# Bias tables, weights and one DMA queue: three edits to a three-layer hybrid network on one core

## The chip, the cores and the metric

The kernel runs on one NeuronCore of a Trainium2 chip. The metric is the device time of one execution in microseconds (us). TensorE (PE) multiplies matrices into eight PSUM banks of 128 partitions by 512 f32 words. VectorE (DVE) and ScalarE (ACT) do the elementwise work, GpSimd (POOL) a little of it, and SyncE (SP) only starts transfers. Transfers run on the core's 16 DMA engines; SP's transfers form one queue (q1 in the profile), POOL's another (q0).

## The reference

Two blocks in a row, on 512 tokens of width 1024 (528 in the first block, which puts 16 meta tokens ahead):

```
layer 0: h += 0.5*swiglu(norm(h)); h += diff_attention(norm(h)) @ w_out; h += 0.5*swiglu(norm(h))
layer 1: the same with dsa_attention: index scores -> top_k keys -> attention on those keys
second block: x += 0.5*swiglu(norm(x))
              x += (ssm branch + dilated attention branch + memory cross attention branch) @ w_out
              x += 0.5*swiglu(norm(x)); out = norm(x)

def _swiglu(x, wi, wo):
    a, b = jnp.split(x @ wi, 2, axis=-1)          # 1024 -> 2 * 2816
    return (jax.nn.silu(a) * b) @ wo

act = relu(einsum("bqhd,bsd->bqhs", qi, k_idx) * IDX_DIM ** -0.5)     # 8 heads of 64
score = einsum("bqh,bqhs->bqs", wi, act)
br_mem = memory_cross_attention(xq, rmsnorm(mem, mem_norm), xattn_w_kv) @ xattn_w_up
```

Both attentions of the first block add a bias that depends on the distance of key and query alone (a table of 16 heads); the dilated attention adds one of 12 heads. There are six swiglu layers in all; they hold most of the work.

## The kernel before

**Precision.** Every f32 operand is split into a high and a low part of type fp32r, and a product of two operands is three matmuls: high by high, low by high, high by low. The split of a weights tile is `loadw` (L82 to L92): SP loads 128x1024 words into `st` (tag "st", three buffers), ACT casts them into `wh` (L89), DVE subtracts to get `wl` (L91).

**A swiglu layer** (`sffn`, L315) has 22 chunks of 128 hidden columns, in four groups of 5, 5, 6 and 6. A chunk's first half needs two products of the input with a 1024x128 slice, one for `a` and one for `b`. Two chunks of the first group are computed plainly (`plain`); the other 20 (`quad`) cut the two products into a 2x2 scheme with seven products of half the depth, 12 matmuls each (L402), 84 in a quad. `a_parts` loads the slices `g` and `u`, `sums` builds the combined weights with DVE additions, and `step(i)` does product i and what follows it. Products 1 and 2 share a PSUM bank, 5 and 3, and 6 and 7; product 4 has its own. ACT copies products 1 and 5 to SBUF (L407, L409), and DVE adds copies and banks (L413, L415, L418, L422, L423), multiplies the two halves (L425), and splits the result into `gh` and `gl`. After the chunks of a group, `partial` (L242) multiplies them with eight tiles of `wo`, one for each 128 output columns (d = 0 to 7): 30 matmuls of 264 columns for a group of five at 528 tokens, 15 of 512 at 512 tokens. The result is added to h by DVE (L262). A `wo` tile of such a group is 128x640 words, 320 KB; a `wi` tile is 512 KB.

**Hooks.** After each of these eight steps a hook may run a piece of another computation, up to its next `yield`: the bias tables `bias_a` (in layer 0's first swiglu, here FFN0) and `bias_d` (in the second block's first, FFN4), and in FFN2 (layer 1's first) the memory norm `mem_norm` and then `ssm_in`. A bias function multiplies the small table with a one-hot matrix (L533, L556), DVE copies the product (L534, L557), POOL stores it to DRAM as `fA` or `fD`, and then POOL starts transfers DRAM to DRAM that write each head's row 128 times, two heads in one transfer: eight `kA<-fA` of 256 rows of 656 words (L538), six `kD<-fD` of 256 rows of 640 words (L562). The attentions later read skewed strips of `kA` and `kD`.

**Banks.** In a swiglu layer, all eight banks form one ring (`s.banks(m=...)`), for products and hooks alike.

**Index scores** (`mixer_b`, L991). Two heads of 64 stand in one tile of 128 partitions; each head's three matmuls contract 64 partitions, on the upper and the lower half of the array.

**Order.** The program is written in the order above; a scheduler with a timing model then orders each engine's instructions at build time, so that pieces of neighbouring chunks, steps and hooks mix. On the chip each engine and each queue keeps that order.

Of the kernel before, what the change touches and what calls it, by code (L numbers as in the profile page):

```python
# [34 lines left out]
class Kern:  # L35
# [278 lines left out]
    def sffn(s, T, x, fi, gnext, final=False, hooks={}, quarters=False, w0=None):  # L314
# [7 lines left out]
        s.banks(m=list(range(8)))  # L322
        with ExitStack() as es:
# [30 lines left out]
            def quad(f):  # L354
# [29 lines left out]
                done = set()  # L384
# [6 lines left out]
                def step(i):  # L391
                    b = bank[i]
                    first = i not in (2, 3, 7)
                    if b not in st:
                        st[b] = s.bank()[:, :N]
                    B = st[b]
                    (wh, wl), o = W[i]
                    c = combo[i]
                    for k in range(4):
                        w = slice(o + k * 128, o + k * 128 + 128)  # L400
                        for z, (a, q) in enumerate(((wh, H), (wh, L), (wl, H))):
                            nc.tensor.matmul(B, a[:, w], q[c][:, k], start=first and k == 0 and z == 0,  # L402
                                             stop=k == 3 and z == 2, skip_group_check=not first)
                    cc = tile("cc", "cc", fp)
                    done.add(i)
                    if i == 1:
                        nc.scalar.copy(cc[:, :N], B)  # L407
                    elif i == 5:
                        nc.scalar.copy(cc[:, 264:264 + N], B)  # L409
                    elif i == 2:  # L410
                        nc.scalar.activation(tile("s", "sl")[:, :N], B, AF.Silu)
                    elif i == 6:
                        v.tensor_add(tile("s", "sl")[:, N:T], B, cc[:, :N])  # L413
                    elif i == 7:
                        v.tensor_add(tile("v", "sq")[:, N:T], B, cc[:, :N])  # L415
                    if i in (6, 3) and {6, 3} <= done:
                        q = st["s"][:, N:T]
                        v.tensor_add(q, st["z"], q)  # L418
                        nc.scalar.activation(q, q, AF.Silu)
                    if i in (7, 4) and {7, 4} <= done:  # L420
                        u = st["v"]
                        v.tensor_add(u[:, :N], st["w"], u[:, N:T])  # L422
                        v.tensor_add(u[:, N:T], u[:, N:T], cc[:, 264:264 + N])  # L423
                    if len(done) == 7:
                        v.tensor_mul(st["s"][:, :T], st["s"][:, :T], st["v"][:, :T])  # L425
                        gate(st["s"][:, :T])
                return a_parts, sums, step
            f0 = 0
            for grp, ng in enumerate((5, 5, 6, 6)):
# [5 lines left out]
                for j in range(2 if grp == 0 else 0, ng):  # L435
# [3 lines left out]
                    for i in (1, 2, 6, 4, 5, 7, 3) if f0 + j == 2 else (1, 6, 4, 5, 2, 7, 3):  # L439
                        step(i)  # L440
# [79 lines left out]
    def bias_a(s):  # L520
# [9 lines left out]
        for q in range(2):  # L530
            p = s.bank()
# [5 lines left out]
        for h in range(0, 16, 2):  # L537
            nc.gpsimd.dma_start(s.kA[h:h + 2], s.fA[h:h + 2].unsqueeze(1).to_broadcast((2, 128, 656)))  # L538

    def bias_d(s):  # L540
# [5 lines left out]
        oh, rt, f = a[:33, :640], a[:33, 640:652], b[:4, :640]  # L546
        nc.vector.memset(rt[32:33], NEG)
        nc.gpsimd.dma_start(rt[:32], s.I["rel_table"])
        for gr in range(3):
            nc.gpsimd.dma_start(oh, s.I["oh2"][:, gr])  # L550
            yield
            yield
            for q in range(2):
                p = s.bank()
                c = slice(q * 320, q * 320 + 320)
                nc.tensor.matmul(p[:4, :320], rt[:, gr * 4:gr * 4 + 4], oh[:, c], start=True, stop=True)  # L556
                nc.vector.tensor_copy(f[:, c], p[:4, :320])  # L557
            nc.gpsimd.dma_start(s.fD[gr * 4:gr * 4 + 4], f)
            yield
        yield  # L560
        for h in range(0, 12, 2):
            nc.gpsimd.dma_start(s.kD[h:h + 2], s.fD[h:h + 2].unsqueeze(1).to_broadcast((2, 128, 640)))  # L562
# [305 lines left out]
    def mixer_b(s, x, gnext, filler=None):  # L868
# [7 lines left out]
        with ExitStack() as es:  # L876
# [21 lines left out]
            with tc.tile_pool(name="bi", bufs=1) as bi:  # L898
                KH, KL = bi.tile([128, 528], F32R, name="kkh"), bi.tile([128, 528], F32R, name="kkl")
# [1086 lines left out]
```

## Time and profile before

| what | value |
|---|---|
| time of the runs, median of 3 | 3423.61 us (3417.93 to 3430.52) |
| time of the profiled execution | 3422.45 us |
| its span, first to last instruction | 3420.7 us |
| busy: PE, weight load, DVE, ACT, POOL | 97%, 90%, 76%, 48%, 8% |
| mean granted clock of TensorE | 0.984 |
| SP's queue, POOL's queue: share of the 16 DMA engines | 29.0%, 2.1% |

The span is what the profile can divide among engines; the 1.75 us between it and the profiled execution's time lie before and after the instructions. Busy shares are averages over stages that differ. A matmul's recorded duration overlaps that of its neighbours, so that the rate of matmuls says more than the busy share. A granted clock of 1.00 is 2.4 GHz, 0.50 is 1.2 GHz.

### The profile page before, as it was taken

What the parts mean: (1) busy time and instruction counts of PE and PEld (TensorE: products, weight loads), DVE (VectorE), ACT (ScalarE), POOL (GpSimd) and SP (SyncE); (2) the same over time, 40 slices, a digit from 0 to 9 for tenths busy, and PEclk for the clock granted to TensorE, in tenths of its full rate; (3) what the DMA queues carried; (4) which work ended last, traced back from release to release, by engine and by line L of the source; (5) the groups of instructions that cost most, each with busy time, mean ns of one, the idle gap of its engine ahead of it and who ended that gap; (6) DMA issues with size and microseconds to landing.
All of it is one profiled execution on the core that took longest, in us unless ns stands there. A gap on an engine that the chain in (4) does not pass through costs nothing. (4 is left out here: it accounts for less than half of the span.)

```text
span 3420.7 us, 60310 instructions
## 1 busy us (share of the span) xinstructions
PE 3304.6 (97%) x23692; PEld 3091.4 (90%) x23692; DVE 2614.7 (76%) x5463; ACT 1645.7 (48%) x3019; POOL 260.0 (8%) x443
## 2 busy tenths in 40 slices
PE   7999999999999999988999999999999899999998
PEld 7999899899999899977989999888998788898998
DVE  8777777799878797778868897787776555387776
ACT  5444577644445344455754444444455534344443
POOL 0100022100000000033310001000000000000000
PEclk9999999999999999999999999999999999999999
DMA  3532322223323433232212333243333243233332
GB/s 132 161 109 82 100 75 70 67 71 120 109 89 102 136 110 106 65 101 75 63 58 89 111 113 118 97 136 112 94 92 96 84 130 96 76 122 103 103 103 62
DMA packets 133646, 336.96 MB, mean 99 GB/s; under 512 B 27043, under 2 KB 39107, under 8 KB 133361
## 3 DMA queue, kind: packets, MB, share of 16 engines
q1 hardware_dynamic: 114336, 311.38, 29.0%
q0 software_dynamic: 19024, 21.72, 2.1%
q8 instruction: 186, 3.05, 0.4%
q14 instruction: 100, 0.81, 0.1%
HBM read 320.00 MB, written 24.35 MB: 101 GB/s over the span
## 5 line engine op out<-in xcount | busy, mean ns | idle before, releaser
L89 ACT CAST wh<-st 128x1024 fp32r<-128x1024 f32 (+5 forms) x385 | 318.9, 840 | 494.8 <-PE bank L111 281.4
L402 PE MATMUL bank<-xh,wh 128*128 128x264 f32 (+1 forms) x1920 | 545.1, 285 | 7.7 <-ACT wh L359 7.7
L402 PE MATMUL bank<-xh,wl 128*128 128x264 f32 (+1 forms) x1920 | 540.7, 284 | 6.8 <-DVE wl L360 6.8
L91 DVE TENSOR_TENSOR wl<-st,wh 128x1024 fp32r<-128x1024 f32 (+4 forms) x373 | 360.9, 974 | 148.0 <-ACT wh L89 146.8
L111 PE MATMUL bank<-gl,wh 128*128 128x264 f32 (+2 forms) x1674 | 456.6, 313 | 0.0
L113 PE MATMUL bank<-gh,wl 128*128 128x264 f32 (+2 forms) x1674 | 453.7, 313 | 0.0
L109 PE MATMUL bank<-gh,wh 128*128 128x264 f32 (+2 forms) x1674 | 453.2, 315 | 0.1
L111 PE MATMUL bank<-xl,wh 128*128 128x264 f32 (+3 forms) x1360 | 426.2, 318 | 4.4 <-DVE xl L182 3.1
L109 PE MATMUL bank<-xh,wh 128*128 128x264 f32 (+3 forms) x1360 | 416.2, 319 | 14.1 <-ACT xh L456 3.2
L113 PE MATMUL bank<-xh,wl 128*128 128x264 f32 (+3 forms) x1360 | 420.9, 315 | 0.0
L402 PE MATMUL bank<-xl,wh 128*128 128x264 f32 (+1 forms) x1440 | 408.2, 284 | 0.0
L402 PEld LDWEIGHTS bank<-xh,wh 128*128 128x128 f32 x1920 | 364.7, 190 | 11.5 <-ACT wh L359 10.3
L402 PEld LDWEIGHTS bank<-xh,wl 128*128 128x128 f32 x1920 | 362.8, 190 | 9.2 <-DVE wl L360 7.9
L402 PE MATMUL bank<-xq,wah 128*128 128x264 f32 (+1 forms) x1920 | 360.8, 284 | 0.3 <-ACT cc L407 0.3
L111 PEld LDWEIGHTS bank<-gl,wh 128*128 128x128 f32 x1674 | 289.1, 189 | 19.3 <-issue 0.5
L109 PEld LDWEIGHTS bank<-gh,wh 128*128 128x128 f32 x1674 | 287.1, 189 | 20.3 <-issue 1.6
L113 PEld LDWEIGHTS bank<-gh,wl 128*128 128x128 f32 x1674 | 287.1, 188 | 19.0 <-DVE wl L91 0.5
L402 PEld LDWEIGHTS bank<-xq,wah 128*128 128x128 f32 x1920 | 298.7, 189 | 1.8 <-ACT cc L407 0.5
L109 PEld LDWEIGHTS bank<-xh,wh 128*128 128x128 f32 (+1 forms) x1360 | 252.4, 190 | 36.2 <-DVE qs L457 4.0
L111 PEld LDWEIGHTS bank<-xl,wh 128*128 128x128 f32 (+1 forms) x1360 | 257.5, 190 | 21.7 <-DVE xl L182 3.8
L402 PEld LDWEIGHTS bank<-xl,wh 128*128 128x128 f32 x1440 | 273.2, 190 | 0.3
L113 PEld LDWEIGHTS bank<-xh,wl 128*128 128x128 f32 (+1 forms) x1360 | 257.0, 190 | 16.7 <-issue 1.4
(597 smaller groups left out, 7534.0 us busy)
## 6 DMA issues: line engine op xcount, KB each, us to landing
st<-in_wi SPq DMA_DIRECT2D x144, 512.0 KB, 4.2
fu<-in_wi SPq DMA_DIRECT2D x120, 512.0 KB, 3.8
st<-in_wo SPq DMA_DIRECT2D x96, 384.0 KB, 3.1
st<-in_wo SPq DMA_DIRECT2D x96, 320.0 KB, 3.0
st<-in_a_w_in SPq DMA_DIRECT2D x24, 512.0 KB, 3.7
st<-in_w_out SPq DMA_DIRECT2D x24, 512.0 KB, 3.7
st<-in_w_g SPq DMA_DIRECT2D x24, 512.0 KB, 3.6
strip<-kA SPq DMA_DIRECT2D x32, 264.0 KB, 2.8
```

Of the source, the lines that this page charges most:

```text
L89: nc.scalar.copy(wh[:rows, :n], st[:rows, :n])
L91: s.wl.tensor_tensor(wl[:rows, :n], st[:rows, :n], wh[:rows, :n].bitcast(F32), op=ALU.subtract)
L109: nc.tensor.matmul(p[:m], a, xh(k, t0, n), start=st, stop=False)
L111: nc.tensor.matmul(p[:m], a, xl(k, t0, n), start=False, stop=False)
L113: nc.tensor.matmul(p[:m], b, xh(k, t0, n), start=False, stop=en)
L402: nc.tensor.matmul(B, a[:, w], q[c][:, k], start=first and k == 0 and z == 0, stop=k == 3 and z == 2, skip_group_check=not first)
```

## The change

**Swiglu.** Products 6 and 7 now accumulate onto a bank ("y") that ACT has filled with a copy of product 1, and product 4 onto a bank ("w") that ACT has filled with a copy of the sum after product 7. In exchange for two more ACT copies, DVE does two additions and two half-width multiplications where it did five additions and one full-width multiplication. The order of products in a chunk becomes 1, 5, 6, 2, 7, 3, 4 (for chunk 2: 1, 2, 5, 6, 3, 7, 4). The ring has seven banks, and the eighth ("k") belongs to the hooks.

**Bias tables.** The `kA<-fA` and `kD<-fD` transfers, and the loads of `bias_d`'s inputs, are started by SP and not by POOL, so that they stand in the weights' queue; there is a `yield` after each pair of heads. **Memory norm.** `mem_norm` moves from FFN2 to FFN0, behind `bias_a`; its loads are SP's too. **Index scores.** The query tile of a head holds the high part in its own half and the low part in the other, so that two matmuls of 128 partitions do what three of 64 did; there are twice as many splits, of 64 partitions each.

```diff
-        s.banks(m=list(range(8)))
+        s.banks(m=list(range(7)), k=[7])
...
                 def step(i):
...
-                    first = i not in (2, 3, 7)
...
+                    B = room(bank[i])
...
+                            first = i in (1, 5) and k == 0 and z == 0
+                            nc.tensor.matmul(B, a[:, w], q[c][:, k], start=first, stop=k == 3 and z == 2,
+                                             skip_group_check=i not in (1, 5))
+                    cc, S, U = tile("cc", "cc", fp), tile("s", "sl"), tile("v", "sq")
                     if i == 1:
+                        nc.scalar.copy(room("y"), B)
+                    elif i == 5:
                         nc.scalar.copy(cc[:, :N], B)
-                    elif i == 5:
+                    elif i == 6:
                         nc.scalar.copy(cc[:, 264:264 + N], B)
                     elif i == 2:
-                        nc.scalar.activation(tile("s", "sl")[:, :N], B, AF.Silu)
-                    elif i == 6:
-                        v.tensor_add(tile("s", "sl")[:, N:T], B, cc[:, :N])
+                        nc.scalar.activation(S[:, :N], B, AF.Silu)
                     elif i == 7:
-                        v.tensor_add(tile("v", "sq")[:, N:T], B, cc[:, :N])
-                    if i in (6, 3) and {6, 3} <= done:
-                        q = st["s"][:, N:T]
-                        v.tensor_add(q, st["z"], q)
-                        nc.scalar.activation(q, q, AF.Silu)
-                    if i in (7, 4) and {7, 4} <= done:
-                        u = st["v"]
-                        v.tensor_add(u[:, :N], st["w"], u[:, N:T])
-                        v.tensor_add(u[:, N:T], u[:, N:T], cc[:, 264:264 + N])
-                    if len(done) == 7:
-                        v.tensor_mul(st["s"][:, :T], st["s"][:, :T], st["v"][:, :T])
-                        gate(st["s"][:, :T])
+                        nc.scalar.copy(room("w"), B)
+                        v.tensor_add(U[:, :N], B, cc[:, :N])
+                    elif i == 3:
+                        v.tensor_add(S[:, N:T], B, cc[:, 264:264 + N])
+                        nc.scalar.activation(S[:, N:T], S[:, N:T], AF.Silu)
+                    elif i == 4:
+                        v.tensor_mul(S[:, :N], B, S[:, :N])
+                        v.tensor_mul(S[:, N:T], S[:, N:T], U[:, :N])
+                        gate(S[:, :T])
...
-                    for i in (1, 2, 6, 4, 5, 7, 3) if f0 + j == 2 else (1, 6, 4, 5, 2, 7, 3):
+                    for i in (1, 2, 5, 6, 3, 7, 4) if f0 + j == 2 else (1, 5, 6, 2, 7, 3, 4):
...
         nc.gpsimd.dma_start(s.fA, f)
         yield
         for h in range(0, 16, 2):
-            nc.gpsimd.dma_start(s.kA[h:h + 2], s.fA[h:h + 2].unsqueeze(1).to_broadcast((2, 128, 656)))
+            nc.sync.dma_start(s.kA[h:h + 2], s.fA[h:h + 2].unsqueeze(1).to_broadcast((2, 128, 656)))
+            yield
...
-        for h in range(0, 12, 2):
-            nc.gpsimd.dma_start(s.kD[h:h + 2], s.fD[h:h + 2].unsqueeze(1).to_broadcast((2, 128, 640)))
+            nc.sync.dma_start(s.kD[h:h + 2], s.fD[h:h + 2].unsqueeze(1).to_broadcast((2, 128, 640)))
...
-                IH, IL = bi.tile([128, 4, 512], F32R, name="qih"), bi.tile([128, 4, 512], F32R, name="qil")
+                IQ = [bi.tile([128, 4, 512], F32R, name="qi%d" % a) for a in range(2)]
...
-                    s.split(IH[:, j], IL[:, j], ac[0][0])
+                    for b, (r, o) in enumerate(HALVES):
+                        s.split(IQ[b][r, j], IQ[b][o, j], ac[0][0][r])
...
-                            for z, (a, b) in enumerate(((IH, KH), (IH, KL), (IL, KH))):
-                                for q in range(2):
-                                    r = slice(q * 64, q * 64 + 64)
-                                    nc.tensor.matmul(ps[q][:, :w], a[r, j, i * 128:i * 128 + 128], b[r, k0:k0 + w],
-                                                     start=z == 0, stop=z == 2)
+                            for q in range(2):
+                                for z, b in enumerate((KH, KL[q])):
+                                    nc.tensor.matmul(ps[q][:, :w], IQ[q][:, j, i * 128:i * 128 + 128], b[:, k0:k0 + w],
+                                                     start=z == 0, stop=z == 1)
...
-            nc.gpsimd.dma_start(m, s.I["memT"][k:k + 2].rearrange("k p n -> p k n"))
+            nc.sync.dma_start(m, s.I["memT"][k:k + 2].rearrange("k p n -> p k n"))
...
-        x = s.sffn(528, x, 0, GI["ln_mix_0"], hooks=spread((0, 7, [s.bias_a()])), w0=w0)
+        x = s.sffn(528, x, 0, GI["ln_mix_0"], hooks=spread((0, 23, [s.bias_a(), s.mem_norm()])), w0=w0)
...
-        x = s.sffn(528, x, 2, GI["ln_mix_1"], hooks=spread((0, 23, [s.mem_norm(), s.ssm_in()])))
+        x = s.sffn(528, x, 2, GI["ln_mix_1"], hooks=spread((0, 23, [s.ssm_in()])))
```

The order of SP's transfers in FFN0, from the second `wo` tile of the first group on. Before, the group's `wo` tiles follow each other (the last six in one row), and the next group's `wi` tiles (`st` and `fu`) come after them:

```order
L367 DMA fu<-in_wi 128x1024
L86 DMA st<-in_wo 128x640
L367 DMA fu<-in_wi 128x1024
L86 DMA st<-in_wo 128x640 x6
L365 DMA st<-in_wi 128x1024 x3
```

Now, from the second `wo` tile on (L1410 loads the memory for `mem_norm`):

```order
L86 DMA st<-in_wo 128x640
L367 DMA fu<-in_wi 128x1024
L86 DMA st<-in_wo 128x640 x2
L536 DMA kA<-fA 256x1x656 x2
L86 DMA st<-in_wo 128x640
L536 DMA kA<-fA 256x1x656 x2
L86 DMA st<-in_wo 128x640
L536 DMA kA<-fA 256x1x656 x3
L86 DMA st<-in_wo 128x640
L536 DMA kA<-fA 256x1x656
L1410 DMA mm<-in_memT 128x2x256 x2
L86 DMA st<-in_wo 128x640
```

All eight tables stand between the `wo` tiles of the first group: two of them ahead of d = 4, four ahead of d = 5, seven ahead of d = 6, all eight ahead of d = 7 and of everything that the second group needs.

The same queue in FFN4, the second block's first swiglu layer, before, from the first `wo` tile:

```order
L86 DMA st<-in_wo 128x640
L367 DMA fu<-in_wi 128x1024
L86 DMA st<-in_wo 128x640
L367 DMA fu<-in_wi 128x1024
L86 DMA st<-in_wo 128x640 x6
```

And now (L563 loads a one-hot matrix):

```order
L86 DMA st<-in_wo 128x640
L367 DMA fu<-in_wi 128x1024
L86 DMA st<-in_wo 128x640
L563 DMA xr<-in_oh 33x640
L566 DMA kD<-fD 256x1x640 x3
L367 DMA fu<-in_wi 128x1024
L566 DMA kD<-fD 256x1x640
L86 DMA st<-in_wo 128x640 x3
L566 DMA kD<-fD 256x1x640 x2
L86 DMA st<-in_wo 128x640 x3
L365 DMA st<-in_wi 128x1024 x3
```

Three tables stand ahead of the last `u` slice of the group, four ahead of d = 2, and all six ahead of d = 5.

The bias products of FFN4 move on PE as well. Before, the first one stands behind 216 product matmuls (L402) of the layer's quads, just ahead of the first `wo` matmuls (L109, L111), and later ones reach into the second group:

```order
L402 MATMUL bank_76<-xh,wl 128x256
L556 MATMUL bank_80<-xr 4x320
L402 MATMUL bank_74<-xh,wh 128x256
L402 MATMUL bank_74<-xl,wh 128x256
L109 MATMUL bank_77<-gh,wh 128x512
```

Now the first product stands behind 52 product matmuls (L404), the second one, shown here, behind 98, and all six ahead of the first `wo` matmul:

```order
L404 MATMUL bank_73<-xh,wl 128x256
L404 MATMUL bank_79<-xh,wh 128x256
L404 MATMUL bank_79<-xl,wh 128x256
L558 MATMUL bank_80<-xr 4x320
L404 MATMUL bank_75<-xh,wh 128x256
```

The tables' transfers can therefore be started earlier in the layer than before.

## Rows read from the trace of the kernel before

**Rows 1.** The page: busy time of the engines, and PE's busy tenths in 40 slices.

```profile
PE 3304.6 (97%) x23692; PEld 3091.4 (90%) x23692; DVE 2614.7 (76%) x5463; ACT 1645.7 (48%) x3019; POOL 260.0 (8%) x443
...
PE   7999999999999999988999999999999899999998
```

**Rows 2.** Windows: us, busy us (instructions) of PE, PEld, DVE, ACT, POOL; clock; DMA.

```profile
100.00:200.00 100.00, 100.00 (x826) 100.00 (x825) 77.18 (x125) 44.34 (x66) 1.07 (x1) 1.00 0.53 163
...
2204.00:2232.00 28.00, 27.08 (x221) 26.09 (x219) 25.73 (x40) 15.26 (x25) 1.05 (x2) 1.00 0.27 82
...
3080.00:3120.00 40.00, 36.18 (x268) 34.27 (x267) 31.47 (x47) 17.80 (x31) 0.00 (x0) 0.96 0.27 85
1080.00:1120.00 40.00, 36.41 (x269) 35.20 (x268) 37.56 (x57) 22.98 (x38) 3.21 (x5) 0.92 0.31 95
```

**Rows 3.** Waits of PE: us in total, times, longest.

```profile
PE bank L402 <- ACT wh L359: 7.7, 9, 1.5
PE bank L402 <- DVE wl L360: 6.8, 5, 1.7
...
PE bank L1334 <- DVE xr L1300: 2.9, 1, 2.9
```

**Rows 4.** DMA issues of the whole span: count, KB each, median us to landing.

```profile
st<-in_wi SPq DMA_DIRECT2D x144, 512.0 KB, 4.2
...
st<-in_wo SPq DMA_DIRECT2D x96, 320.0 KB, 3.0
...
kA<-fA POOLq DMA_DIRECT2D x8, 656.0 KB, 25.2
...
kD<-fD POOLq DMA_DIRECT2D x6, 640.0 KB, 19.7
...
fA<-xr POOLq DMA_DIRECT2D x1, 41.0 KB, 1.9
```

**Rows 5.** DMA queues from 2248 to 2251 us: packets, MB, share of 16 engines.

```profile
q0 software_dynamic: 43, 0.22, 17.7%
q1 hardware_dynamic: 32, 0.07, 7.0%
```

**Rows 6.** DMA queues from 97 to 108 us.

```profile
q0 software_dynamic: 1950, 2.15, 60.3%
```

**Rows 7.** DMA issues from 2242.1 to 2244 us.

```profile
st<-in_wo SPq DMA_DIRECT2D x1, 320.0 KB, 7.2
```

**Rows 8.** Timeline of POOL around both tables: start, us, instruction, wait before it.

```profile
90.31 7.46 POOL L538 DMA_DIRECT2D kA<-fA  x7 [1.68 <-DMA fA<-xr]
...
2240.30 1.13 POOL L562 DMA_DIRECT2D kD<-fD  x1 [2.61 <-DMA fD<-xr]
2242.49 1.08 POOL L562 DMA_DIRECT2D kD<-fD  x1 [1.07 <-issue]
```

**Rows 9.** Timeline of SP from 76 to 112 us.

```profile
77.15 16.81 SPq L86 DMA_DIRECT2D st<-in_wo  x6
```

**Rows 10.** Timeline of ACT from 74 us: the cast of FFN0's third quad's last weights.

```profile
74.41 1.06 ACT L359 CAST wh<-st 128x1024 fp32r<-128x1024 f32 x1 [0.98 <-DVE st L379]
```

**Rows 11.** Timelines of DVE: last additions to h of the first group, FFN0 and FFN4.

```profile
109.94 0.76 DVE L262 SCALAR_TENSOR_TENSOR h<-bank,h 128x264 f32<-128x264 f32 x2
...
2267.45 0.68 DVE L262 SCALAR_TENSOR_TENSOR h<-bank,h 128x512 f32<-128x512 f32 x1
```

**Rows 12.** Timeline of PE: FFN4's first bias products.

```profile
2231.65 0.70 PE L556 MATMUL bank<-xr 33*4 33x320 f32 x2
```

**Rows 13.** Groups of DVE and ACT in the quads: count, busy us, mean ns, idle before.

```profile
L413 DVE TENSOR_TENSOR sl<-bank,cc 128x264 f32<-128x264 f32 (+1 forms) x120 | 50.9, 425 | 19.0 <-PE bank L402 18.0 <-ACT gh L456 0.8
...
L425 DVE TENSOR_TENSOR sl<-sl,sq 128x528 f32<-128x528 f32 (+1 forms) x120 | 83.0, 693 | 1.1
...
L407 ACT COPY cc<-bank 128x264 f32<-128x264 f32 x60 | 22.7, 379 | 67.0 <-PE bank L402 64.5 <-DVE sq L423 2.3
```

**Rows 14.** Timeline of PE in the index scores.

```profile
1484.92 0.41 PE L111 MATMUL bank<-xl,wh 128*128 128x264 f32 x2
1485.26 0.40 PE L991 MATMUL bank<-kkh,qih 64*128 64x264 f32 x2
1485.49 0.29 PE L991 MATMUL bank<-kkl,qih 64*128 64x264 f32 x2
```

More of the change, by code (lines that the diff above doesn't have):

```diff
@@ L383, in quad, with room @@
                 bank = {1: "x", 2: "x", 3: "z", 4: "w", 5: "z", 6: "y", 7: "y"}
-                done = set()
+                def room(b):
+                    if b not in st:
+                        st[b] = s.bank()[:, :N]
+                    return st[b]
                 def tile(nm, tag, pool=s.tmp, **kw):
@@ L545, in bias_d @@
         a, b = s.scratch()
-        oh, rt, f = a[:33, :640], a[:33, 640:652], b[:4, :640]
+        ohs, rt = (a[:33, :640], b[:33, :640]), a[:33, 640:652]
         nc.vector.memset(rt[32:33], NEG)
-        nc.gpsimd.dma_start(rt[:32], s.I["rel_table"])
+        nc.sync.dma_start(rt[:32], s.I["rel_table"])
+        for gr in range(2):
+            nc.sync.dma_start(ohs[gr], s.I["oh2"][:, gr])
+        yield
+        yield
         for gr in range(3):
-            nc.gpsimd.dma_start(oh, s.I["oh2"][:, gr])
             yield
@@ L553, in bias_d @@
             for q in range(2):
-                p = s.bank()
+                p = s.bank("k")
                 c = slice(q * 320, q * 320 + 320)
-                nc.tensor.matmul(p[:4, :320], rt[:, gr * 4:gr * 4 + 4], oh[:, c], start=True, stop=True)
-                nc.vector.tensor_copy(f[:, c], p[:4, :320])
-            nc.gpsimd.dma_start(s.fD[gr * 4:gr * 4 + 4], f)
+                nc.tensor.matmul(p[:4, :320], rt[:, gr * 4:gr * 4 + 4], ohs[gr % 2][:, c], start=True, stop=True)
+                f = s.t528("ra", "fd")[:4, :320]
+                nc.vector.tensor_copy(f, p[:4, :320])
+                nc.gpsimd.dma_start(s.fD[gr * 4:gr * 4 + 4, c], f)
+            if gr == 0:
+                nc.sync.dma_start(ohs[0], s.I["oh2"][:, 2])
+        for h in range(0, 12, 2):
             yield
-        yield
-        for h in range(0, 12, 2):
-            nc.gpsimd.dma_start(s.kD[h:h + 2], s.fD[h:h + 2].unsqueeze(1).to_broadcast((2, 128, 640)))
+            nc.sync.dma_start(s.kD[h:h + 2], s.fD[h:h + 2].unsqueeze(1).to_broadcast((2, 128, 640)))
     def strip(s, pool, src, row, n, tag, mask=True):
@@ L1375, in ssm_out @@
             yield
-            p = s.bank()
+            p = s.bank("k")
             for a in range(4):
```

31 lines of the change are left out of this document (15 added, 16 removed).

## The prediction

> **What bounds the kernel now.** I began with the page [rows 1]. PE is busy 97% of the span and only the first and the last of 40 slices are below 8 tenths, so time can be gained only where PE stands still or runs at a low clock. The table of windows shows which engine sets the pace inside a swiglu layer [rows 2]: from 100 to 200 us PE starts 826 matmuls at a granted clock of 1.00, .121 us for each of 264 columns, while DVE is busy 77 us and ACT 44. In FFN4, 221 matmuls in 28 us give .127 us. So in the middle of a layer PE is the bound, and work taken from DVE there is worth nothing by itself. The starts of layers differ: 1080 to 1120 and 3080 to 3120 us ran at clocks of .92 and .96, with PE busy 36 of 40 us. PE's waits say why [rows 3]: products (L402) wait 7.7 us in nine places for high halves of weights, 6.8 us in five for low halves, and one transpose of FFN2 waits 2.9 us. That is all that the swiglu edits could win: 14.5 + 2.9 us, and the lost clock behind it (40 x .08 = 3.2 us and 40 x .04 = 1.6 us in the two windows; 2.4 us over five later starts is 12), 29 us at most.
>
> Then I looked at the transfers, since the change puts some megabytes of them into the queue on which PE's weights come. The list of DMA issues [rows 4] shows what is unusual: a `wi` tile of 512 KB lands 4.2 us after its issue, a `wo` tile of 320 KB after 3.0, but a `kA` transfer of 656 KB after 25.2 and a `kD` of 640 KB after 19.7. The queues from 2248 to 2251 us say where that comes from [rows 5]. Two `kD` transfers and what was left of a weights tile are under way, and both queues together take 17.7 + 7.0 = 24.7% of 16 engines, about four. So each table goes over two engines. POOL's queue moved .22 MB in .177 x 16 x 3 = 8.5 engine-us, 25.9 GB/s for each engine. A `kD` transfer (655,360 bytes) is then 655,360 / 2 / 25.9 GB/s = 12.65 us on two engines, a `kA` (671,744) 13.0 us; a weights tile of 320 KB over all sixteen is .79 us, and 256 KB of the memory .63.
>
> Before, this slowness is hidden. With several `kA` in flight from 97 to 108 us POOL's queue fills 60.3% of the engines [rows 6], 9.6 of them: different transfers use different pairs. The six last `wo` tiles of FFN0's first group go out on SP's queue meanwhile [rows 9], and one beside the `kD` transfers lands after 7.2 us in place of 3.0 [rows 7], which its prefetch covers.
>
> **The tables on SP's queue.** The transfer keeps its shape, so I keep two engines and 25.9 GB/s each. What no row tells is which two. I choose that on SP's queue each transfer takes the same two: POOL takes about 1.1 us to issue one [rows 8], enough to choose engines anew each time, and nothing in the rows shows such a step on SP. Then the eight (or six) stand one behind the other, and since each weights tile has a sixteenth on every engine, a tile behind a table in the queue lands only when that table has.
>
> The Trainium skill speaks for this choice. "DMA: Bandwidth & Descriptors", section "Why a DMA increments its semaphore by 16 and not by 1", gives the engine count as the largest number up to 16 that divides the slowest dimension of both sides, and says that the hardware queue takes the lowest-numbered ones each time where POOL's goes round; by that the tables have two engines and always the same. On POOL's queue the trace agrees (24.7% with two in flight [rows 5], 60.3% with several [rows 6]); no run here shows it on SP's.
>
> *FFN0.* The first `kA` needs `fA`, hence DVE's second copy. I put it right behind the low half of the third quad's last weights, whose cast runs from 74.4 to 75.5 us [rows 10]: about 77 us, and with 1.9 us for the store [rows 4] and the issue the first table starts near 80. Eight take 8 x 13.0 = 104 us, the four `wo` tiles d = 4 to 7 among them 4 x .79 = 3.2, two memory loads 1.3: the last tile is through at 188.5, and 2 us later it is landed and cast, at 190.5. Before, the last additions to h of this group end at 109.94 + .76 = 110.7 [rows 11], so the matmuls of d = 7 began 30 x .121 us sooner, at 107.1. PE has nothing else to do: the next group's weights stand behind the same tables. The end moves by 190.5 - 107.1 = **+83 us**, whatever its division among d = 4 to 7.
>
> *FFN4.* The first bias product on PE ran at 2231.65 [rows 12]. Now the second stands behind 98 product matmuls, which from about 2204.2 and at .1276 us each are done at 2216.7. Copy, store (2.5 us by `fD`'s likes) and issue put the first `kD` near 2221. Six take 6 x 12.65 = 76 us, to 2297; with a `u` slice, three `wo` tiles (1.3 + 3 x .79) and 2 to 3 us of landing and cast d = 5 can start at about 2304. Before, d = 7 ended its addition at 2267.45 + .68 [rows 11]; three times 15 matmuls of .22 us back from 2267 is 2257. So **+47 us**. The move of POOL's loads of `rel_table` and one-hot matrices to SP adds three of some 80 KB, .2 us each: nothing. Nor is anything won on POOL, which waits for no one there and for whom no engine waits (its 7.46 us of seven issues [rows 8]).
>
> After each of these two idles PE comes back at half clock and the following group starts with no prefetched weights; I take 2 us each, **+4 us**, from the 3.2 and 1.6 us lost at layer starts above.
>
> **The swiglu edits.** Per quad DVE does five additions of 425 ns and one multiplication of 693 [rows 13] before, and four operations of 425 after: -1.1 us; ACT does two copies of 379 ns more, +.76 us. With PE the bound both are worth 0 in the middle of a layer. The new dependence is that products 6, 7 and 4 wait for an ACT copy into their bank. What covers it is the product in between (5 between 1 and 6, 3 between 7 and 4): 12 x .121 = 1.45 us, against .38 us of copy. Without that cover each would cost up to .4 us, 120 x .4 = 48 us; only chunk 2 puts its order differently, and there 2 and 5, and 3, still lie between. At layer starts I take half of the 29 us, **-15 us**: less DVE work ahead of the low halves and no memory norm in FFN2; but ACT, which the high halves wait for, has more, so from +20 to -29. The memory norm in FFN0 gives its work to engines with room; its loads are in the sum above.
>
> **Index scores.** Before, a pair of 64-row matmuls takes one slot of .12 us, and .34 us (1485.26 to .40 behind an L111 matmul) at a switch of kinds [rows 14]. 120 such in 60 slots become 80 of 128 rows: 20 x .13 = +2.7 us, fewer switches back: **+1**, -4 to +5, with the doubled splits (some 2.5 us on ACT and DVE each) beside PE's work.
>
> **Sum.** 83 + 47 + 4 - 15 + 1 = +120 on the profiled execution's 3422.45 us, which is 1.2 below the median of the runs: 3542 us.
>
> **The rivals.** *A, the other side: the queue doesn't matter.* If SP's queue spreads a table over all engines, 656 KB are 1.6 us and the queue hardly notices. For it: SP's tiles of other shapes land in 3 to 4 us [rows 4], and a transfer's engines may belong to the queue and not to the shape. Against it: the shape is the same one that gave two engines. It decides as soon as a table takes less than about 4 us, for then eight tables in some 27 us fit into the prefetch. The time is 3422 - 15 + 1 = 3408, with the whole 29 us of starts 3394.
>
> *B, two engines, another pair each time.* Then tables run beside each other as on POOL's queue, and a weights tile waits for one table, about 13 us once in each place and mostly within the prefetch of some 15 us; +5 us on A: 3413.
>
> *C, slower tables.* On the same two engines always, and with each transfer as long as its landing on POOL's queue took [rows 4]: 8 x (25.2 - 13.0) = +98 and 6 x (19.7 - 12.65) = +42 us, 3682. Against it: those times include sharing engines with other tables, which one at a time doesn't do.
>
> *D, ACT as the new limit.* If the added copies stand behind weights' casts in ACT's order, products 6, 7 and 4 wait. For it: ACT's casts are already the last to end at starts [rows 3]. Against it: ACT has 56 of 100 us free [rows 2]. It would add up to 1 us in some 25 quads at starts, 3422 + 25 = 3447 without the tables' stall.
>
> **How the numbers follow.** The main case has .68, A .14, B .07, C .07, D alone .04. The main case itself reaches from 3470 (the tables start 10 us sooner in each place, 30% faster, and 29 us of starts) to 3640 (23 GB/s, 2 us lost at more starts and +20 there). Without the upper half of C and the lower part of A the range is 3405 to 3650. About 0.5%, 17 us, is what a measurement here can tell from no change. Faster by more than that, under 3406.5, is nearly half of A with a little of B; the same, the rest of both and part of D: .09 and .13. Slower: .78.
>
> **What would show it.** In the changed profile, if I am right: two dark stretches in PE's slices, near 100 to 190 and 2240 to 2304 us; in the list of waits PE's `wo` matmuls (L109, L111) behind casts of weights that wait for `st<-in_wo`; a median or some landing times of `wo` tiles in tens of us; DMA shares near two engines' (12%) there with `kA` and `kD` on q1. The quads' rate elsewhere stays at .121 us. Wrong, if the tables land in a few us, or overlap on q1 with more than two engines; then the swiglu edits are all that counts. Wrong in size, if a table alone takes other than 13 us. D shows as waits of L404 for ACT's copies into banks (L408, L416).

## The result, and the profile after

The changed kernel takes 3568.3 us (median of 4 runs, 3565.72 to 3570.33), the kernel before 3420.8 beside it: the ratio is 1.0429, with a 95% interval of 1.0417 to 1.0442. 145 to 148 us were lost where 119 were forecast (from 3423 to 3542). The profiled execution has a span of 3566.8 us.

The page of the changed kernel first, busy time of the engines, then PE's busy tenths and its granted clock in 40 slices of 89 us, against [rows 1]:

```profile
PE 3313.3 (93%) x23652; PEld 3097.6 (87%) x23652; DVE 2515.9 (71%) x5228; ACT 1713.7 (48%) x3263; POOL 240.1 (7%) x421
...
PE   7189999999999999988999999949999999999998
...
PEclk9699999999999999998999999979999999999999
```

Two holes appear, in the second slice (89 to 178 us) and in the 27th (2318 to 2408 us). PE is busy nearly as long as before, 3313 us for 3305: of the 146 us by which the span grew it stands still in 137. The waits of PE say for what (us in total, times, longest; compare [rows 3]):

```profile
PE bank L109 <- ACT wh L89: 134.4, 11, 33.0
...
PE bank L404 <- ACT wh L359: 5.3, 8, 1.5
...
PE bank L404 <- DVE wl L360: 3.4, 3, 1.9
```

The first row is new: `wo` products wait for casts of `wo` tiles. Four waits of 84 us in all lie before 205 us, two of 49 us in FFN4. The waits of quads' products on weights fell from 14.5 to 8.7 us. What the casts wait for is seen in SP's own timeline around the first hole (start, us for the rows grouped in a line, instruction, count; compare [rows 9]):

```profile
73.28 1.46 SPq L86 DMA_DIRECT2D st<-in_wo  x2
76.94 6.67 SPq L536 DMA_DIRECT2D kA<-fA  x2
83.72 12.96 SPq L86 DMA_DIRECT2D st<-in_wo  x1
96.73 14.95 SPq L536 DMA_DIRECT2D kA<-fA  x2
111.78 13.29 SPq L86 DMA_DIRECT2D st<-in_wo  x1
125.13 27.55 SPq L536 DMA_DIRECT2D kA<-fA  x3
152.77 13.32 SPq L86 DMA_DIRECT2D st<-in_wo  x1
166.14 0.84 SPq L536 DMA_DIRECT2D kA<-fA  x1
167.02 15.71 SPq L1410 DMA_DIRECT2D mm<-in_memT  x2
182.83 1.59 SPq L86 DMA_DIRECT2D st<-in_wo  x1
```

Even the act of starting a transfer is slow here: issuing one `wo` tile takes 13 us where it takes .3 elsewhere, once two tables are on their way. What a table costs in the queue is the step from its first packet to the next table's: by the trace 13.5 to 13.6 us, 14.4 where a `wo` tile stands between, and 15.0 for the first. The queue itself, from 140 to 150 us, with nothing but a table in it (packets, MB, share of 16 engines; compare [rows 5, 6]):

```profile
q1 hardware_dynamic: 192, 0.50, 13.0%
```

13.0% of sixteen is 2.1 engines, and .50 MB in 10 us is 50 GB/s, 24 for each. From the first packet of the tables to the last (78.4 to 190.7 us) never more than four of them are under way at once, two for 101 of the 112 us: the tables stand one behind the other. The landings of a weights tile's parts say where it waits. Of the sixteen that the trace has of the `wo` tile issued at 83.7 us, fourteen come at 98.8 to 99.2 us and two at 108.2 and 108.3, 0.7 us after the two of the table ahead: two of its sixteenths stood behind the table. The windows of both stretches (columns as in [rows 2]):

```profile
100.00:200.00 100.00, 21.13 (x120) 20.27 (x121) 11.81 (x22) 7.20 (x9) 0.00 (x0) 0.59 0.23 78
2300.00:2420.00 120.00, 71.31 (x429) 60.39 (x428) 48.37 (x76) 29.96 (x49) 3.07 (x6) 0.80 0.26 88
```

From 100 to 200 us PE issued 120 matmuls, at a mean clock of .59, where it had issued 826. The last additions to h of the two groups, against [rows 11]:

```profile
202.84 0.76 DVE L262 SCALAR_TENSOR_TENSOR h<-bank,h 128x264 f32<-128x264 f32 x2
...
2419.17 0.69 DVE L262 SCALAR_TENSOR_TENSOR h<-bank,h 128x512 f32<-128x512 f32 x1 [1.19 <-PE bank L113]
```

FFN0's group ends at 203.6 for 110.7, 92.9 us later. FFN4 starts 99.9 us later than before (its first product at 2304.1 for 2204.2) and its group ends 151.7 later, so 51.8 us were lost in it.

### The profile page after: what moved, and what is told of

Same layout as the page of the kernel before. It is cut to its first block, busy times and chain, and to the rows that moved or that the text cites. A ratio compares the mean times of both kernels' runs of the same rounds, so it can differ in the third digit from the quotient of the medians.

```text
span 3566.8 us, 60086 instructions
## 1 busy us (share of the span) xinstructions
PE 3313.3 (93%) x23652; PEld 3097.6 (87%) x23652; DVE 2515.9 (71%) x5228; ACT 1713.7 (48%) x3263; POOL 240.1 (7%) x421
## 4 chain that ended last, share of the span: by engine, by line
PE 74%; issue 8%; DVE 8%; DMA 4%; ACT 3%; SPq 3%; POOL 1%; DVEq 0%; ACTq 0%; POOLq 0%
PE bank L404 28%; PE bank L109 13%; PE bank L111 12%; PE bank L113 12%; PE bank L1112 2%; DMA st<-in_wo 1%; SPq L536 1%; DMA mm<-in_memT 1%; SPq L86 1%; PE bank L1531 1%; PE bank L1128 1%; PE bank L1739 1%; DVE wl L91 1%; PE bank L828 1%; ACT wh L89 0%
## 5 line engine op out<-in xcount | busy, mean ns | idle before, releaser
L109 PE MATMUL bank<-gh,wh 128*128 128x264 f32 (+2 forms) x1674 | 459.4, 317 | 133.9 <-ACT wh L89 133.5
L404 PE MATMUL bank<-xh,wh 128*128 128x264 f32 (+1 forms) x1920 | 544.9, 285 | 5.9 <-ACT wh L359 5.3
L404 PE MATMUL bank<-xh,wl 128*128 128x264 f32 (+1 forms) x1920 | 536.2, 284 | 3.5 <-DVE wl L360 3.4
L111 PE MATMUL bank<-gl,wh 128*128 128x264 f32 (+2 forms) x1674 | 463.0, 314 | 0.0
L109 PE MATMUL bank<-xh,wh 128*128 128x264 f32 (+3 forms) x1360 | 415.3, 318 | 16.8 <-DVE qs L455 2.8
L109 PEld LDWEIGHTS bank<-gh,wh 128*128 128x128 f32 x1674 | 290.8, 190 | 156.3 <-ACT wh L89 139.1
L111 PE MATMUL bank<-xl,wh 128*128 128x264 f32 (+3 forms) x1360 | 423.7, 316 | 1.8 <-DVE xl L182 1.8
L404 PE MATMUL bank<-xl,wh 128*128 128x264 f32 (+1 forms) x1440 | 408.0, 284 | 0.0
L404 PEld LDWEIGHTS bank<-xh,wh 128*128 128x128 f32 x1920 | 364.1, 190 | 12.2 <-ACT wh L359 7.6
L404 PEld LDWEIGHTS bank<-xh,wl 128*128 128x128 f32 x1920 | 360.5, 190 | 5.9 <-DVE wl L360 4.8
L404 PE MATMUL bank<-xq,wah 128*128 128x264 f32 (+1 forms) x1920 | 362.2, 284 | 1.3 <-ACT bank L408 1.3
L111 PEld LDWEIGHTS bank<-gl,wh 128*128 128x128 f32 x1674 | 292.9, 190 | 18.2
L113 PEld LDWEIGHTS bank<-gh,wl 128*128 128x128 f32 x1674 | 291.0, 190 | 18.4 <-DVE wl L91 0.4
L404 PEld LDWEIGHTS bank<-xq,wah 128*128 128x128 f32 x1920 | 298.7, 189 | 3.0 <-ACT bank L408 1.9
L109 PEld LDWEIGHTS bank<-xh,wh 128*128 128x128 f32 (+1 forms) x1360 | 250.5, 189 | 39.5 <-DVE qs L455 3.9
L404 PEld LDWEIGHTS bank<-xl,wh 128*128 128x128 f32 x1440 | 273.4, 190 | 0.8
L111 PEld LDWEIGHTS bank<-xl,wh 128*128 128x128 f32 (+1 forms) x1360 | 255.7, 189 | 18.5 <-DVE xl L182 2.2
L404 PE MATMUL bank<-xq,wal 128*128 128x264 f32 (+1 forms) x960 | 270.9, 282 | 0.0
```

Source lines behind the costliest of these rows:

```text
L109: nc.tensor.matmul(p[:m], a, xh(k, t0, n), start=st, stop=False)
L111: nc.tensor.matmul(p[:m], a, xl(k, t0, n), start=False, stop=False)
L113: nc.tensor.matmul(p[:m], b, xh(k, t0, n), start=False, stop=en)
L404: nc.tensor.matmul(B, a[:, w], q[c][:, k], start=first, stop=k == 3 and z == 2, skip_group_check=i not in (1, 5))
```

## Where the time lies, stretch by stretch

This table is worked out from the traces: a layer F0 to F5 runs from its first product of a quad to its last `wo` matmul, F3-4 is the stretch between FFN3 and FFN4 (the norm and the plain chunks), and F2-3 the second mixer, with the index scores. The kernels under the second row are the experiments below; the stretches that are left out differ by at most 5 us.

```
                        F0     F1     F2   F2-3     F3   F3-4     F4     F5   span
before               335.9  333.2  355.8  399.8  335.7   28.5  334.7  329.2  3420.7
changed              431.1  338.6  343.6  400.5  338.2   37.3  381.5  327.3  3566.8
e1 tables on POOL    345.8  337.0  344.0  396.0  337.1   35.0  339.6  329.0  3430.1
e2 rows outermost    340.6  339.2  344.0  395.6  338.2   36.1  329.3  327.3  3418.7
e4 four heads        382.1  339.1  342.4  400.7  338.2   35.1  344.7  327.3  3483.2
e5 tables on ACT     429.4  338.6  342.4  397.8  337.1   35.3  369.4  327.6  3547.0
e6 old quads         339.4  334.2  343.0  391.2  336.5   28.7  331.3  325.6  3396.8
e7 memory in FFN2    335.7  338.6  347.8  393.9  337.0   35.7  332.0  327.6  3420.9
e8 old index scores  341.7  339.1  342.7  401.6  338.2   34.6  332.8  327.3  3428.0
e9 ring of eight     346.3  335.4  341.2  395.0  341.2   36.8  331.4  329.5  3430.7
e10 order alone      341.8  335.2  340.7  395.9  336.2   28.8  331.4  325.5  3401.3
e11 quads alone      338.7  338.6  346.9  398.3  338.2   36.0  336.2  327.4  3431.2
e12 best parts?      337.2  335.1  345.5  396.1  337.4   28.6  329.9  325.6  3404.8
```

## The experiments: the tables

The theory is the prediction's: a table uses as many engines as it has heads in a transfer, on SP's queue always the same ones, and the weights behind it in that queue wait.

**Tables on POOL's queue again**, all else as changed:

```diff
-            nc.sync.dma_start(s.kA[h:h + 2], s.fA[h:h + 2].unsqueeze(1).to_broadcast((2, 128, 656)))
+            nc.gpsimd.dma_start(s.kA[h:h + 2], s.fA[h:h + 2].unsqueeze(1).to_broadcast((2, 128, 656)))
```

(and the same line for `kD`)

> The changed kernel, with the kA and kD transfers started by POOL again and nothing else undone. Theory (tables on two engines stand one behind the other in the weights' queue): both dark stretches go, 89 us in FFN0's first group and 47 to 56 around FFN4's, so 3423 to 3432 us, and the six wo tiles of the first group land in under 10 us each. Rival (the swiglu edits, the seven-bank ring or the memory norm in FFN0 make the stretches): above 3520 us, with PE still waiting tens of us at the first group's wo products.

It took 3433.7 us (ratio to before 1.0036, 1.0023 to 1.0049). Both holes are gone, F0 from 431 to 346 us and F4 from 382 to 340. The tables take about as long as before to land (DMA issues: KB, us to landing; compare [rows 4]):

```profile
kA<-fA POOLq DMA_DIRECT2D x8, 656.0 KB, 22.8
```

So the holes come from the tables in the weights' queue; that the swiglu edits or the hooks make them is out. The time is just above the range expected, and 10 us above that of the next run, in which the tables are quick (F0 is 5 us longer, F4 10). Something stands behind the tables on POOL's queue as well: the small stores `fD<-fd`. In FFN4 DVE waits for one of them, its split of `wo` weights comes after that, and PE waits 7.4 us for the split (DVE's timeline, then PE's waits of the whole run, with the longest last):

```profile
2254.31 0.48 DVE L560 COPY fd<-bank 4x320 f32<-4x320 f32 x1 [12.94 <-DMA fD<-fd]
```

```profile
PE bank L113 <- DVE wl L91: 8.4, 5, 7.4
```

**The same places on SP's queue, with the rows outermost:**

```diff
-            nc.sync.dma_start(s.kA[h:h + 2], s.fA[h:h + 2].unsqueeze(1).to_broadcast((2, 128, 656)))
+            nc.sync.dma_start(s.kA[h:h + 2].rearrange("h p n -> p h n"),
+                              s.fA[h:h + 2].unsqueeze(0).to_broadcast((128, 2, 656)))
```

(and so for `kD`)

> The changed kernel, with the tables still on SP's queue, in the same places between the same weights, but each transfer written with the 128 rows as its outermost dimension and the two heads inside. Theory (two heads outermost confine a transfer to two engines, 12.7 to 13.0 us each): the transfers take all sixteen engines, 1.6 us each by bytes, all eight are through within 20 us of the first and the stalls are gone: 3422 to 3435 us. Rival (a copy from DRAM to DRAM in the weights' queue is slow whatever its shape): within 20 us of the changed kernel's 3568.

3423.3 us, ratio 1.0002 (.9993 to 1.0011). SP's transfers stand in the same order as in the changed kernel; only the shape differs. The queue from 79 to 104 us, and the issues in it:

```profile
q1 hardware_dynamic: 3390, 7.48, 91.4%
...
kA<-fA SPq DMA_DIRECT2D x8, 656.0 KB, 12.6
st<-in_wo SPq DMA_DIRECT2D x4, 320.0 KB, 10.7
```

The queue moves 7.48 MB in 25 us, 299 GB/s over nearly all engines where the two-engine tables had moved 50. A table still lands 12.6 us after its issue, since eight of them with weights are started within 10 us and share the engines, but all eight are through by 103 us, 24 us after the start of the first (20 were expected), which the prefetch covers; F4 is 52 us shorter than in the changed kernel. That a copy from DRAM to DRAM is slow by itself is out: the cost is the shape.

**Four heads in a transfer:**

```diff
-        for h in range(0, 16, 2):
-            nc.sync.dma_start(s.kA[h:h + 2], s.fA[h:h + 2].unsqueeze(1).to_broadcast((2, 128, 656)))
+        for h in range(0, 16, 4):
+            nc.sync.dma_start(s.kA[h:h + 4], s.fA[h:h + 4].unsqueeze(1).to_broadcast((4, 128, 656)))
```

> The changed kernel, with four heads in a transfer instead of two: the same bytes in half as many transfers. Theory (as many engines as heads, always the lowest ones): four engines, a transfer still takes 13 us, so the tables are through in 4 x 13.0 = 52 us for 104 and 3 x 12.65 = 38 us for 76: 90 us less stall, about 3478 us. Rival (the queue moves such copies at some 52 GB/s whatever the number of engines): 26 us for a transfer and about 3568 us.

One run gave 3485.2 us, 7 us above the theory's time and 83 below the rival's. F0 is 49.0 us shorter than in the changed kernel, F4 36.8, where 52 and 38 were expected. From 100 to 106 us, with only a table in the queue:

```profile
q1 hardware_dynamic: 228, 0.60, 26.1%
```

26.1% is 4.2 engines, and .60 MB in 6 us is 100 GB/s: twice the heads, twice the engines, twice the rate. This step between two and sixteen is what makes the rule on heads and engines more than a guess.

**Tables on ACT's queue:**

```diff
-            nc.sync.dma_start(s.kA[h:h + 2], s.fA[h:h + 2].unsqueeze(1).to_broadcast((2, 128, 656)))
+            nc.scalar.dma_start(s.kA[h:h + 2], s.fA[h:h + 2].unsqueeze(1).to_broadcast((2, 128, 656)))
```

> The changed kernel, with the kA and kD transfers started by ACT, whose queue is another one than the weights'. Theory (a weights tile waits because it stands behind a table in the same queue, not because two engines are busy): weights land in under 10 us beside the tables, and what is lost is what ACT loses while it starts them, under 40 us: 3425 to 3470 us. Rival (weights wait because the two engines are busy with tables): their sixteenths on these two engines wait as before, above 3520 us.

3548.8 us in one run: by its time the rival's. The trace says otherwise. From 96 to 102 us, after a `wo` tile was issued at 96.47 beside the running tables, the queues moved:

```profile
q1 hardware_dynamic: 144, 0.33, 19.1%
q10 hardware_dynamic: 98, 0.26, 11.1%
```

The .33 MB of q1 are that tile; q10 is ACT's queue. Fourteen of its sixteen landings come by 99.2 us and the last two at 102.2, 5.8 us after its issue: two engines busy with tables hold the last parts of a weights tile up by 3 us, where a table ahead in its own queue held up those of d = 4 to 6 by 8.5 to 9.1 us in the changed kernel, after an issue of 13. What keeps PE waiting is ACT itself (its timeline):

```profile
86.43 14.02 ACTq L536 DMA_DIRECT2D kA<-fA  x1
86.64 0.71 ACT L89 CAST wh<-st 128x640 fp32r<-128x640 f32 x1
100.49 26.77 ACTq L536 DMA_DIRECT2D kA<-fA  x2
127.31 0.36 ACT L416 COPY bank<-bank 128x264 f32<-128x264 f32 x1 [39.95 <-issue]
```

From the third table on each issue holds ACT for 13.3 to 14.1 us, as SP was held, and no cast is started meanwhile: 40 us of idle ACT between two instructions. PE's two longest waits are for such instructions:

```profile
PE bank L404 <- ACT bank L416: 39.4, 3, 38.9
PE bank L109 <- ACT gh L454: 35.2, 1, 35.2
```

The theory's queue holds, but its price for ACT, under 40 us, was wrong by far, since I had not thought that starting a transfer could wait for an earlier one.

## The experiments: the other edits

With the rows outermost (e2) the tables are out of the way and the sum of the other edits was to show: -14 us by the prediction, +1.5 by the measurement (3423.3 for 3421.8), which cannot be told from none. So each was taken out of that kernel.

**The quads as before** (step and order of products of the kernel before, the rest as in e2):

```diff
-                    if i == 1:
-                        nc.scalar.copy(room("y"), B)
...
+                    if i in (7, 4) and {7, 4} <= done:
+                        u = st["v"]
+                        v.tensor_add(u[:, :N], st["w"], u[:, N:T])
...
-                    for i in (1, 2, 5, 6, 3, 7, 4) if f0 + j == 2 else (1, 5, 6, 2, 7, 3, 4):
+                    for i in (1, 2, 6, 4, 5, 7, 3) if f0 + j == 2 else (1, 6, 4, 5, 2, 7, 3):
```

> The kernel with the rows outermost (3423 us), with the order and the additions of the quads as before the change, all else as changed. Theory Q (the added ACT copies and the new order make weights and copies late in the middle of layers; FFN1's 334 us became 339 there and FFN0's later groups lost 6): FFN1 is back at 333 to 334 us and the time is 3405 to 3414. Rival (the seven-bank ring or the hooks do it, the quads nothing): FFN1 stays at 338 to 340 us and the time at 3420 to 3427.

3400.4 us, ratio .9942 (.9928 to .9955), below both ranges: the quads' edit costs 23 us by the times and 21 by the ratios, and without it the kernel is faster than before. In the table F1 falls from 339.2 to 334.2 and F3-4 from 36.1 to 28.7.

**The new order of products with the old additions** splits the edit:

```diff
-                    for i in (1, 2, 6, 4, 5, 7, 3) if f0 + j == 2 else (1, 6, 4, 5, 2, 7, 3):
+                    for i in (1, 2, 5, 6, 3, 7, 4) if f0 + j == 2 else (1, 5, 6, 2, 7, 3, 4):
```

(against e6)

> The kernel with the quads of before and the rows outermost (3400 us), with one thing of the quads' edit put back: the order 1, 5, 6, 2, 7, 3, 4 of the products (1, 2, 5, 6, 3, 7, 4 in chunk 2); the additions stay DVE's. Theory A (the 23 us that the quads' edit costs come from the copies of ACT into banks): 3397 to 3406 us. Theory B (they come from the order of the products, that is of the weights they need): 3415 to 3428.

3400.9 us (.9943, .9931 to .9955). The order is free; the copies into banks and the accumulation onto them, which replace DVE's additions, cost the 22 us. Windows of 300 us in FFN1, of e10:

```profile
728.00:1028.00 300.00, 298.86 (x2452) 298.07 (x2452) 264.28 (x627) 129.57 (x204) 6.19 (x16) 1.00 0.33 102
```

and of e2, with the copies:

```profile
728.00:1028.00 300.00, 296.66 (x2419) 294.49 (x2418) 245.62 (x581) 140.96 (x242) 6.19 (x16) 1.00 0.32 102
```

DVE has 18.7 us less to do, ACT 11.4 more, and PE starts 33 matmuls fewer, 4 us at .122. PE's longest waits in the whole of FFN1 in e2, where the kernel before has none:

```profile
PE bank L404 <- ACT wh L359: 1.5, 2, 0.8
PE bank L404 <- DVE wl L360: 0.9, 1, 0.9
PE bank L404 <- ACT cc L412: 0.5, 1, 0.5
```

They are waits for weights above all, which ACT casts in the same order of instructions as the copies. From the start of a product matmul (L404) to that of the next matmul, five steps are longer than .45 us, where the kernel before has none; they hold 3.9 us more than five ordinary ones. The mean of the rest is .1228 us for .1217, 1.8 us over 1674: together 5.7 of FFN1's 6 us. Over the whole kernel the product matmuls wait for weights and for copies into banks as follows in e2

```profile
PE bank L404 <- ACT wh L359: 6.2, 8, 2.1
...
PE bank L404 <- DVE wl L360: 3.4, 3, 1.9
...
PE bank L404 <- ACT bank L408: 1.5, 2, 0.9
```

and for weights in e6, which has no such copies:

```profile
PE bank L402 <- ACT wh L359: 4.0, 6, 1.4
...
PE bank L402 <- DVE wl L360: 1.5, 3, 0.7
```

So late weights are 4.1 of the 22 us. Late copies (with .4 us of L416) are 1.9, about what the products lose to other waits in e6 (2.2). At the start of FFN4 two waits of the norm stand in every kernel with the copies, which are 0.6 and 1.1 us in the kernel before (e2, from 2174 us):

```profile
PE bank L109 <- ACT xq L214: 3.5, 1, 3.5
PE bank L111 <- DVE xq L215: 3.2, 1, 3.2
```

with a mean clock of .86 from 2174 to 2210 us, where the kernel before had 1.00 from 2175.7 to 2204.2. Presumably it is the order that the build-time scheduler gives to the norm's pieces; that, and why the copies should move it, is not shown. FFN1 and this stretch hold 11 to 12 of the 22 us, and the rest lies spread over other stretches, without one wait that accounts for it.

**The quads' edit alone, on the kernel before:**

```diff
-        s.banks(m=list(range(8)))
+        s.banks(m=list(range(7)), k=[7])
...
+                    if i == 1:
+                        nc.scalar.copy(room("y"), B)
```

> The kernel before, with the quads' edit alone (copies into banks, the new order, seven banks for products and one for hooks). Theory Q (the edit costs some 23 us wherever it stands): 3438 to 3450 us. Rival (the 23 us were the build-time order of that one kernel, which every edit shuffles): within 8 us of before's 3422. The prediction's term for this edit, -15 us, would be 3407.

3438.4 us, ratio 1.0048 (1.0035 to 1.0061): +18 us, on another kernel and with another order of everything around. F1 is 338.6 and F3-4 36.0 again. So it is not one unlucky order. (The profiled execution is the fastest of the five, so the table shows 10.5 of the 18 us.)

**All eight banks in one ring** (against e2):

```diff
-        s.banks(m=list(range(7)), k=[7])
+        s.banks(m=list(range(8)))
```

> The kernel with the rows outermost (3423 us), with all eight banks in one ring again for products and hooks. Theory Q (quads, not banks): within 4 us of 3423, FFN1 at 337 to 340 us. Rival (a ring of seven makes products wait): FFN1 back at 333 to 335 us and the time 3408 to 3416.

3433.5 us (1.0036, 1.0024 to 1.0048), 10 us slower than e2 and outside both expectations: F1 gains 3.8, as the rival has it, but F0 loses 5.7 and F3 3.0. So the ring of seven is not what costs in the whole; its part in FFN1 stays open. This kernel does not compute the reference's values, for a cause that is open; it has as many instructions on each engine as the changed kernel, and only its time is read.

**The memory norm back in FFN2** (against e2):

```diff
-hooks=spread((0, 23, [s.bias_a(), s.mem_norm()])), w0=w0)
+hooks=spread((0, 7, [s.bias_a()])), w0=w0)
...
-hooks=spread((0, 23, [s.ssm_in()])))
+hooks=spread((0, 23, [s.mem_norm(), s.ssm_in()])))
```

> The kernel with the rows outermost (3423 us), with the memory norm back in FFN2. Theory (the 12 us that FFN2 gained are the memory norm's, and FFN0's later groups pay at most half of them back): FFN2 344 to 354 us, FFN0 0 to 6 shorter, the time 3427 to 3436. Rival (FFN2 gained from the quads): FFN2 stays below 347 us and the time at 3417 to 3424.

3420.3 us (.9999, .9990 to 1.0007), by its time the rival's. F2 loses 3.8 of the 12 us and F0 gains 4.9 back: what the move is worth here cannot be told from nothing, and most of FFN2's gain is due to other edits than it. In the table FFN2 with the memory norm in it takes 345.5 to 347.8 us in the three kernels in which the hooks have a bank of their own (e7, e11, e12) and 355.8 in the kernel before, in which they share the ring. So that bank may be what FFN2 gained from; no run changes it alone. **The same on the kernel with the old quads** (e6), whose edit is that diff once more:

> The kernel with the quads of before and the rows outermost (3400 us), with the memory norm back in FFN2. If the move of the memory norm is worth nothing or costs (3423 became 3420 without it): 3394 to 3402 us. If it is worth the 12 us that FFN2 gained: 3408 to 3414.

3409.5 us (.9967, .9958 to .9977), within the second range: there the move is worth 9 us. So the move is worth next to nothing beside the quads' edit and 9 us without it; why is not shown. The best kernels measured are e6 and e10, which are alike.

**The index scores as before** (64 rows, three matmuls; against e2):

```diff
-                            for q in range(2):
-                                for z, b in enumerate((KH, KL[q])):
...
+                            for z, (a, b) in enumerate(((IH, KH), (IH, KL), (IL, KH))):
+                                for q in range(2):
```

> The kernel with the rows outermost (3423 us), with the index scores in 64 rows as before. Prediction (+1 us for the edit): 3419 to 3424. Rival (the edit took the 4 us that the stretch between FFN2 and FFN3 lost, 399.8 to 395.6): that stretch is back at 399 to 401 us and the time at 3426 to 3429.

3433.2 us (1.0035, 1.0022 to 1.0047), above all that was expected: the edit gains 10 us, where +1 was predicted and at most -4 allowed. The time in which an index-score matmul runs, worked out from the traces, is 17.3 us with 80 of 128 rows (e2), and 18.4 (before) and 19.0 (e8) with 120 of 64: 1 to 2 us less, where the prediction had 1 more. The gain lies in two stretches, 6.0 us in F2-3, which holds the index scores, and 3.5 in F4, which the edit touches only by the order of what is around it; I did not find one wait that accounts for it, and that stays open.

## Why the prediction was right, and where not

- **The bound, the two engines, the same pair, one behind the other: right**, and shown by e1, e2 and e4, not only by the trace after. The Trainium skill's statement on the engine count and on the lowest-numbered engines (page "DMA: Bandwidth & Descriptors", section "Why a DMA increments its semaphore by 16 and not by 1") agrees with all three on its first half: 2.1 engines with two heads, 4.2 with four, over 90% with 128 rows outermost. That they are the same ones each time is what two packets under way for 101 of 112 us, the 13.5 us from table to table and the two late sixteenths of a `wo` tile say; their numbers no run here shows. Rivals A, B and C are out.
- **FFN0, +83 us: 89.4 on PE, 90.5 by e2's trace.** The first product behind the group starts at 200.02 us for 110.58; the 92.9 us between the last additions hold 3.5 us more, in which DVE was late and PE worked on. The step that failed is the price of a table: 13.5 us where the sum has 13.0, which rests on 3 us of `kD` transfers (in FFN4 a `kD` did take 12.7 to 12.8 us where nothing stood between). The tables started at 78.4 for 80 and were through at 190.7 for 186.4, tiles among them included. The last `wo` tile landed with them, at 193.25, and ACT, which had the squares of the memory norm (L1418) behind it by then, cast it at once:

```profile
191.88 1.26 ACT L1418 ACTIVATE mm<-mm 128x512 f32<-128x512 f32 x2 [13.47 <-DMA mm<-in_memT]
193.35 0.72 ACT L89 CAST wh<-st 128x640 fp32r<-128x640 f32 x1 [0.21 <-DMA st<-in_wo]
```

  So d = 7 began at 194.1 for 190.5. Its first 18 matmuls ran at .22 us each (half clock) until 198.4, 2.3 us more than at full clock, for the 2 of the sum.
- **FFN4, +47 us: 52.1 on PE, 52.2 by e2, 51.8 by the additions.** d = 5 began when forecast: 2304 and the 99.9 us by which the layer starts later are 2403.9.

```profile
2404.05 0.79 PE L109 MATMUL bank<-gh,wh 128*128 128x512 f32 x1 [15.64 <-ACT wh L89]
```

  The tables and the tiles among them took 81 us (2321.3 to 2402.4), where the sum has 80. The step that failed is what was left to do: 58 `wo` products came from there on, where the sum has 45, and in the kernel before the same 58 began at 2252.6 and not at 2257. They took 0.6 us longer than there, where 2 stood for the restart. Tables together: 134 us predicted, 145 measured (3568.3 - 3423.3).
- **The swiglu edits, -15 us: wrong in sign.** They cost 21 to 23 us (e6), 18 on the kernel before (e11). The step that failed is the cover: I priced a copy by its own .38 us against the 1.45 us of the product in between and put ACT's added work at nothing since ACT is busy 44% of the time. The copies and the accumulation onto them cost the 22 us (e10). How they do it is shown in part: later weights, which ACT casts in one order with the copies, are 4 us of it, copies that come late (the mechanism of rival D) at most 2, and the stretch ahead of FFN4 holds 7; the rest is open. The waits of products for weights did fall, from 14.5 to 8.7 us, but they fell to 5.5 with the quads as before (e6), so what was won there is not this edit's alone.
- **Index scores, +1: -10 in the kernel's time**, with the matmuls themselves within 3 us of the prediction; the gain has no shown cause.
- **The move of the memory norm**, whose work the sum has at nothing: not to be told from nothing beside the quads' edit, -9 us without it. Its squares held up no cast in FFN0's hole.

The sum is 26 us short, 11 of them in the tables and 15.5 in the other edits, which came to +1.5 where -14 was written. That they came to no more is luck: the quads' +22 and some -21 of the rest nearly cancel, and neither stands in the sum.

## What to carry to other kernels

Before a transfer is put into the queue that feeds the critical engine, look at its share of the engines in the profile and at its outermost dimension: the same bytes at the same place cost 145 us more with the two heads outermost than with the 128 rows. A slow transfer may stand in a queue that nothing urgent shares (on POOL's even a small store behind the tables cost 7 us), but not be started by an engine with other work. And "the engine has room" prices an edit on its mean; where that engine also feeds the bound, an edit that relieves an engine off the path can cost more than it wins.

## What was not expected of the hardware

Starting a transfer can itself take as long as the transfer ahead: on SP a `wo` tile's issue took 12.96 to 13.32 us behind two tables for .33 elsewhere, on ACT a table's 13.3 to 14.1 (e5). On POOL seven tables of the same size were issued in 7.46 us [rows 8], though they landed some 25 us later. So in these runs the engine that starts pays on these two queues and not on POOL's. And a tile on SP's queue landed 5.8 us after its issue beside tables on ACT's (e5), but 24.6 us after it behind tables on its own.
